# First head's k projected in the adaLN stage of a hybrid GLA and SSD layer

## The chip, the cores and the metric

The kernel runs on one core of a Trainium2 chip. The metric is the device time of one execution in microseconds; a profile is one execution recorded instruction by instruction. The engines are TensorE (PE, with its weight loads as PEld), VectorE (DVE), ScalarE (ACT), GpSimd (POOL) and the DMA queues; SyncE (SP) issues most transfers.

## The reference

One layer of a diffusion backbone over 512 latent tokens and 256 context tokens, width 1024, all in float32:

```
ada   = silu(c) @ w_ada + b_ada                    # six vectors of 1024; the same for c_ctx
h     = rms_norm(x) * (1 + scale1) + shift1        # context: its own scale and shift
parts = h @ w_in                                   # q, k, v, r, low-rank gates, z, xs, B, C, dt, gates a and b
y_a   = gated linear attention, both directions, 4 heads (dk 128, dv 256) @ w_pa
y_b   = Mamba-2 SSD, both directions, 32 heads in 4 groups @ w_pb
x     = x + g1 * ((sigmoid(gate_a)*y_a + sigmoid(gate_b)*y_b) @ w_out)
out   = rms_norm(x + g2 * swiglu(modulated rms_norm(x)))
```

The scans of the latent tokens start from the final states of the context tokens.

## The kernel before, in words

Every matrix product is done in three passes with operands split into a high and a low part: high by high, high by low, low by high. A weight block of 128x1024 comes by `load_w(key)`: SP loads it into one of three `raw` buffers (`load_raw`, line 176), ACT writes the high part `whi` (line 188), and DVE, later POOL, the low part `wlo` (line 189). `whi` and `wlo` have two buffers each. The names in a profile carry the key: `whi_k` is the high part of a head's k weights.

The start (lines 225 to 318) uses a pool `st`. The input x is normalised and transposed into `xnT`. The adaLN weights for shift1 and scale1 come in four blocks b of two loads `aw` of 1 MB each. `ada_first(b)` sums a block on PE (line 277, bank `ada`), copies it to `ar` on ACT (line 280) and turns it with four matmuls (line 283, bank `adaT`). `h_of(b)` then writes the normalised input's parts `hH` (ACT, line 299) and `hL` (DVE, line 301) for the contraction tiles 2b and 2b+1. The weights of `misc` (low-rank gates and dt) and of the first head's q are loaded ahead here, without priority.

When `st` is closed, the pools `pj` and `ch` are opened and take over its memory.

`proj_cols(key, with_ctx)` projects one 128-column block: for each of the eight contraction tiles three matmuls of 512 latent columns (lines 361, 362, 366, result `l_...`) and, with context, three of 256 columns (lines 364, 365, 368, result `c_...`). The results lie in banks of the tag `mm`, of which there are four; the tag `sm` has four more. `proj_rows` does v, r and z (lines 386 to 388, results `r_v`, `r_r`, `r_z`).

In program order, misc is projected first and copied into `M` (lines 394 to 398). From `M` and the small matrix `U` (read through `early_in`, a DMA of POOL, line 403) come the split operands `MS` (lines 413 to 415). The gate matmuls `pre` (line 469) follow, then the log-sigmoid `ge` on ACT and DVE (lines 471 to 474), its split `gh` and `gl` (lines 477, 478), and their way through DRAM (`gdr`). The dt values and their sums come next, and only then `gla_proj(0)`: q, k, v and r of head 0.

For each head h `gla_chain` runs the attention on the gates (`gc`, `kx`, `ky`, states `S`, levels `lv`, masks into `att`, outputs `o`, turned ones `oT`), while the projections of head h+1 fill PE between its steps. The chain's matmuls have high priority. Between the chains of heads 1 and 2, and again before that of head 3, `early_gate()` projects a pair of output gates (`l_ga`, `l_gb`) and writes them (`tg`) to DRAM (`tdr`). The four SSD groups follow, then the remaining output gates near 900 us, w_out and the FFN.

The other adaLN blocks (16 to 39 of 48, 128 columns each) are summed on POOL: `some_ada()` is called at certain weight blocks; every second call loads a block into a `raw` buffer (`raw_ada`) and POOL multiplies and adds it (lines 341 to 345); a one-column matmul ends it (line 336). Blocks that are left over run in the gate projections near 900 us.

The order of the instructions on each engine is fixed when the program is built, by a list scheduler that takes the first ready instruction in order of priority; each engine then runs its list in order and waits where an operand isn't there. `tc.high_priority()` lifts a part. `tc.issue_after(ins)` puts what is written inside it behind `ins` in the queue of its engine.

Of the kernel before, what the change touches and what calls it, by code (L numbers as in the profile page):

```python
# [14 lines left out]
P = 128  # L15
# [114 lines left out]
def hybrid_layer_kernel(ctx: ExitStack, tc: tile.TileContext, x, xc, wts, vec, rows, up, msk, lvl, out):  # L130
# [94 lines left out]
    with tc.tile_pool(name="st", bufs=1) as st:  # L225
        tcs = st.tile([P, KD, 2], F32, name="tcs")
        craw = vecs[:, V_CS:V_CS + 16].rearrange("p (k j) -> p k j", j=2)
        nc.scalar.activation(tcs, craw, AF.Tanh, scale=0.5)

        pre_ln = tc.keep_in_program_order(nc.scalar.preload_act_table_set("natural_log_exp_and_others"))  # L230
        nc.vector.scalar_tensor_tensor(cs, tcs, 1.0, craw, ALU.add, ALU.mult)
        nc.vector.tensor_scalar(cs, cs, 0.5, None, ALU.mult)

        csw = st.tile([P, KD, 32], F32, name="csw")
        nc.gpsimd.memset(csw, 0.0)
        nc.gpsimd.tensor_copy(csw[:, :, 0:2], cs)
        xs_ = [st.tile([P, D], F32, name=f"xt_{i}") for i in range(6)]
        xnT = st.tile([P, KD, NT], F32, name="xnT")
        mk = st.tile([P, M_TOT, P], F32, name="mk")

        def load_aw(b):
            ts = []
            for i in range(2):
                n = WIDX[("ada0", b, 2 * i)]
                raw = st.tile([P, 4, 512], F32, tag="aw", name=f"aw_{b}_{i}", bufs=6)
                nc.sync.dma_start(raw.rearrange("p (j k) c -> p j (k c)", j=2), wts[n:n + 2].rearrange("j p c -> p j c"))
                ts.append(raw)
            return ts

        def load_x(i):  # L250
            nc.sync.dma_start(xs_[i], x[i * P:(i + 1) * P, :] if i < 4 else xc[(i - 4) * P:(i - 3) * P, :])

        aw = [None] * 4
        nc.sync.dma_start(mk, msk)
        nc.vector.tensor_copy(idt, mk[:, M_ID, :])
        nc.gpsimd.tensor_copy(mkr, mk[:, 1:6, :])
        nc.gpsimd.tensor_copy(le8, mk[:, M_LE, :])

        sel = st.tile([P, 2], F32, name="sel")
        nc.vector.tensor_tensor(sel, mk[:, M_ID, 0:2], mk[:, M_ID, 32:34], ALU.add)  # L260
        for q in (64, 96):
            nc.vector.tensor_tensor(sel, sel, mk[:, M_ID, q:q + 2], ALU.add)
        for i in range(6):
            load_x(i)
        for b in range(4):
            aw[b] = load_aw(b)
        in_start[0] = True
        for key in (("misc",), ("q", 0)):
            ahead[key] = load_w(key)
        in_start[0] = False  # L270

        def ada_first(b):
            pt = sm_bank(f"ada_{b}")

            for k in range(KD):
                q = slice(32 * (k % 4), 32 * (k % 4) + 32)
                nc.tensor.matmul(pt[q, :], csw[:, k, :], aw[b][k // 4][:, k % 4, :], start=(k < 4), stop=(k >= 4))
            with tc.high_priority():
                ar = st.tile([P, 512], F32, tag="ar", name=f"ar_{b}", bufs=2)
                nc.scalar.activation(ar, pt, AF.Copy)  # L280
                pt = sm_bank(f"adaT_{b}")
                for j in range(4):
                    nc.tensor.matmul(pt[:, 2 * j:2 * j + 2], ar[:, j * P:(j + 1) * P], sel, start=True, stop=True)
                pv = pt[:, 0:8].rearrange("p (c j t) -> p c j t", c=2, t=2)
                k0 = 2 * b
                for c in range(2):
                    j0 = 8 * c + k0
                    nc.vector.tensor_tensor(ada[:, j0:j0 + 2, :], pv[:, c],
                                            vecs[:, V_BADA + j0:V_BADA + j0 + 2].unsqueeze(2).to_broadcast([P, 2, 2]), ALU.add)

                nc.vector.scalar_tensor_tensor(
                    s1[:, k0:k0 + 2, :], ada[:, 8 + k0:10 + k0, :], 1.0,
                    vecs[:, V_N1 + k0:V_N1 + k0 + 2].unsqueeze(2).to_broadcast([P, 2, 2]), ALU.add, ALU.mult)

        def h_of(b):
            for k in (2 * b, 2 * b + 1):
                for w, t0, n in ((0, 0, SEQ), (1, SEQ, CTX)):
                    xv = xnT[:, k, t0:t0 + n]
                    nc.scalar.activation(hH[:, k, t0:t0 + n], xv, AF.Identity, bias=ada[:, k, w:w + 1], scale=s1[:, k, w:w + 1])
                    nc.vector.tensor_scalar(xv, xv, s1[:, k, w:w + 1], ada[:, k, w:w + 1], ALU.mult, ALU.add)  # L300
                nc.vector.tensor_tensor(hL[:, k, :], xnT[:, k, :], hH[:, k, :].bitcast(F32), ALU.subtract)

        for i in range(6):
            sq = st.tile([P, D], F32, tag="sq", name=f"xsq_{i}")
            ss = sml.tile([P, 1], F32, tag="ss", name=f"xss_{i}", bufs=4)
            nc.scalar.activation(sq, xs_[i], AF.Square, accum_out=ss)
            r = rstd_of(ss, D, f"x{i}")
            nc.vector.tensor_scalar(xs_[i], xs_[i], r, None, ALU.mult)
            for half in range(2):
                pt = sm_bank(f"xT_{i}_{half}")  # L310
                for k in range(4):
                    kk = half * 4 + k
                    nc.tensor.transpose(pt[:, k * P:(k + 1) * P], xs_[i][:, kk * P:(kk + 1) * P], ident)
                nc.scalar.activation(xnT[:, half * 4:half * 4 + 4, i * P:(i + 1) * P],
                                     pt.rearrange("p (k t) -> p k t", t=P), AF.Copy)
        for b in range(4):
            ada_first(b)
            h_of(b)
# [30 lines left out]
    def proj_cols(key, with_ctx):  # L349
        if key[0] in ("q", "k") and key[1:2] != (0,):  # L350
            for _ in range(2):
                some_ada()
        if key[0] in ("ga", "gb"):
            some_ada()
        hi, lo = load_w(key)
        nm = "_".join(map(str, key))
        lat = mm_bank("l_" + nm)
        cx = mm_bank("c_" + nm) if with_ctx else None
        for k in range(KD):
            st, sp = k == 0, k == KD - 1  # L360
            nc.tensor.matmul(lat, hi[:, k, :], hH[:, k, 0:SEQ], start=st, stop=False)
            nc.tensor.matmul(lat, hi[:, k, :], hL[:, k, 0:SEQ], start=False, stop=False)
            if with_ctx:
                nc.tensor.matmul(cx[:, 0:CTX], hi[:, k, :], hH[:, k, SEQ:NT], start=st, stop=False)
                nc.tensor.matmul(cx[:, 0:CTX], hi[:, k, :], hL[:, k, SEQ:NT], start=False, stop=False)
            nc.tensor.matmul(lat, lo[:, k, :], hH[:, k, 0:SEQ], start=False, stop=sp)
            if with_ctx:
                nc.tensor.matmul(cx[:, 0:CTX], lo[:, k, :], hH[:, k, SEQ:NT], start=False, stop=sp)
        return lat, cx


    def proj_rows(keyf, ntile):
        banks = [mm_bank(f"r_{'_'.join(map(str, keyf(0)))}_{b}") for b in range(ntile // 2)]
        for kh in range(2):
            hi, lo = load_w(keyf(kh))
            if keyf(0)[0] in "vr":
                some_ada()
                some_ada()
            for i in range(ntile):
# [9 lines left out]
        return banks  # L389


    lat, cx = proj_cols(("misc",), True)
    M = pj.tile([P, NT], F32, tag="cva", name="M")
    nc.vector.memset(M[0:64, :], 1.0)
    for src, t0, n in ((lat, 0, SEQ), (cx, SEQ, CTX)):
# [26 lines left out]

    gnh = rsm[:, R_GN:R_GN + DV]
    nc.vector.tensor_scalar(gnh, gnh, 0.5, None, ALU.mult)


    def gla_proj_qk(h):
        lat, _ = proj_cols(("q", h), False)
        qT = pj.tile([P, SEQ], F32, tag="p3", name=f"qT_{h}")
        nc.scalar.activation(qT, lat, AF.Copy, scale=float(DK) ** -0.5)  # L430
        big = pj.tile([P, 3072], F32, tag="x12", name=f"kv_{h}")
        vt = big[:, 0:1536].rearrange("p (i c) -> p i c", c=DV)
        kt = big[:, 1536:2304].rearrange("p (i c) -> p i c", c=DK)
        kT = big[:, 2304:3072]
        lat, cx = proj_cols(("k", h), True)
        nc.scalar.activation(kT[:, 0:SEQ], lat, AF.Copy)
        nc.vector.tensor_copy(kT[:, SEQ:NT], cx[:, 0:CTX])
        for b, i0, n in ((0, 0, 4), (1, 4, 2)):
            pt = sm_bank(f"kt_{h}_{b}")
            for i in range(n):  # L440
                nc.tensor.transpose(pt[:, i * P:(i + 1) * P], kT[:, (i0 + i) * P:(i0 + i + 1) * P], ident)
            nc.scalar.activation(kt[:, i0:i0 + n, :], pt[:, 0:n * P].rearrange("p (i c) -> p i c", c=DK), AF.Copy)
        return qT, vt, kt, kT

    def gla_proj_vr(h, qT, vt, kt, kT):
        banks = proj_rows(lambda kh: ("v", h, kh), 6)
# [118 lines left out]
        nc.gpsimd.dma_start(cdr[d].rearrange("i h t -> (i h) t"), ct)  # L565
    ecum = cst.tile([P, 2, 4, 32], F32, name="ecum")
    nc.scalar.activation(ecum, cum, AF.Exp)
    pr = gla_proj(0)


    class Early:
# [643 lines left out]
```

## Time and profile before

| what | value |
|---|---|
| median of three runs | 1433.0 us (1431.25 to 1437.1) |
| profiled execution, its own time | 1428.55 us |
| its span, first to last instruction | 1426.7 us |
| PE busy | 1349.4 us, 95% |
| DVE, ACT, POOL busy | 881.1, 496.7, 476.1 us |
| mean granted clock of TensorE | 0.986 |

The profile's times count from the first instruction of the span. Busy time is a sum over instructions; an engine that is not on the chain that ends last may be idle at no cost.

### The profile page before, as it was taken

To read this page: it belongs to the slowest core of one execution; us is meant where nothing else is said; L and a number is where in the kernel's file an instruction comes from. 1 tells how busy PE (TensorE), PEld (TensorE's weight loads), DVE (VectorE), ACT (ScalarE), POOL (GpSimd) and SP (SyncE) were. 2 spreads that over 40 slices of the span, in tenths; PEclk is the share of its full clock that TensorE was granted. 3 is DMA by queue.
4 is the path that set the end of the run, shared out by engine and by line. 5 is a ranking of instruction groups with operands and counts; after the bars stand their busy time and mean duration, and the time that the engine had idled before them with its cause. 6 is when DMAs were issued, how large, how long until landed. Compare 5 with 4: busy or idle time off the path is not lost.

```text
span 1426.7 us, 19130 instructions
## 1 busy us (share of the span) xinstructions
PE 1349.4 (95%) x7462; PEld 1146.0 (80%) x7462; DVE 881.1 (62%) x1317; ACT 496.7 (35%) x825; POOL 476.1 (33%) x341
## 2 busy tenths in 40 slices
PE   5888999999998999998999989999889999999997
PEld 3687999889888778876887787778678888888886
DVE  4599757583595588558857975767683343433235
ACT  6464343433434132532332342332333323232222
POOL 1346555245423533343353324114641122100001
PEclk9998999999999999999999999999999999999999
DMA  9375433423422423323322333457423343333331
GB/s 370 123 259 151 128 102 111 126 93 126 122 75 67 141 98 101 97 73 90 104 82 89 96 97 101 158 184 267 135 87 109 113 122 115 120 116 93 100 106 72
DMA packets 71386, 175.49 MB, mean 123 GB/s; under 512 B 6384, under 2 KB 22912, under 8 KB 71168
## 3 DMA queue, kind: packets, MB, share of 16 engines
q1 hardware_dynamic: 57056, 161.11, 34.6%
q0 software_dynamic: 13952, 12.79, 3.8%
q8 instruction: 59, 0.97, 0.3%
q10 hardware_dynamic: 288, 0.36, 0.1%
q14 instruction: 31, 0.25, 0.1%
HBM read 159.37 MB, written 14.87 MB: 122 GB/s over the span
## 4 chain that ended last, share of the span: by engine, by line
PE 66%; DVE 16%; DMA 9%; issue 5%; ACT 2%; POOL 1%; SPq 0%; POOLq 0%; DVEq 0%; ACTq 0%
DMA E<-cdr 6%; PE up L1069 3%; PE gate L1068 3%; PE gate L1069 3%; PE up L1068 3%; PE gate L1067 3%; PE up L1067 3%; DVE E L830 3%; PE db L204 3%; PE db L206 3%; PE db L205 3%; PE lv L577 2%; PE pb_pb L716 2%; PE pb_pb L715 2%; PE pb_pb L717 2%
## 5 line engine op out<-in xcount | busy, mean ns | idle before, releaser
L341 POOL TENSOR_TENSOR raw_ada<-raw_ada,cs 128x1024 f32<-128x1024 f32 x32 | 69.7, 2180 | 265.3 <-DMA raw_ada<-in_wts_dram 230.4
L830 DVE TENSOR_TENSOR E<-E,ebias 128x512 f32<-128x512 f32 x64 | 68.8, 1077 | 51.0 <-DMA E<-cdr 50.8
L343 POOL TENSOR_TENSOR raw_ada<-raw_ada 128x512 f32<-128x512 f32 x64 | 80.0, 1250 | 3.7
L386 PE MATMUL r_z<-whi_z,hH 128*128 128x256 f32 x256 | 74.6, 291 | 5.8 <-DVE z L781 3.0
L388 PE MATMUL r_z<-whi_z,hL 128*128 128x256 f32 x256 | 73.4, 287 | 0.0
L387 PE MATMUL r_z<-wlo_z,hH 128*128 128x256 f32 x256 | 73.0, 285 | 0.0
L1067 PE MATMUL gate<-h2H,whi_gate 128*128 128x512 f32 (+1 forms) x192 | 72.2, 376 | 0.0
L1068 PE MATMUL gate<-h2L,whi_gate 128*128 128x512 f32 (+1 forms) x192 | 72.1, 376 | 0.0
L1069 PE MATMUL gate<-h2H,wlo_gate 128*128 128x512 f32 (+1 forms) x192 | 71.9, 374 | 0.0
L189 POOL TENSOR_TENSOR wlo_xs<-raw_xs,whi_xs 128x1024 fp32r<-128x1024 f32 x16 | 40.6, 2536 | 75.3 <-ACT whi_xs L188 75.3
L1069 PE MATMUL up<-h2H,wlo_up 128*128 128x512 f32 x160 | 63.0, 394 | 0.0
L1068 PE MATMUL up<-h2L,whi_up 128*128 128x512 f32 x160 | 62.4, 390 | 0.0
L1067 PE MATMUL up<-h2H,whi_up 128*128 128x512 f32 x160 | 62.3, 389 | 0.0
L189 DVE TENSOR_TENSOR wlo_down<-raw_down,whi_down 128x1024 fp32r<-128x1024 f32 x18 | 22.1, 1225 | 62.4 <-ACT whi_down L188 62.3
L189 DVE TENSOR_TENSOR wlo_gate<-raw_gate,whi_gate 128x1024 fp32r<-128x1024 f32 x20 | 31.7, 1584 | 45.6 <-ACT whi_gate L188 45.6
L170 POOL TENSOR_TENSOR rr_f<-rv_f,negh 128x1 f32<-128x1 f32 x4 | 2.6, 662 | 168.5 <-DVE rv_f L168 168.5
L386 PE MATMUL r_v<-whi_v,hH 128*128 128x256 f32 x192 | 56.4, 294 | 0.0
L189 POOL TENSOR_TENSOR wlo_z<-raw_z,whi_z 128x1024 fp32r<-128x1024 f32 x16 | 39.6, 2475 | 49.2 <-ACT whi_z L188 36.6
L387 PE MATMUL r_v<-wlo_v,hH 128*128 128x256 f32 x192 | 55.5, 289 | 0.0
L715 PE MATMUL pb_pb<-yT,whi_pb 128*128 128x512 f32 x128 | 55.3, 434 | 0.0
L388 PE MATMUL r_v<-whi_v,hL 128*128 128x256 f32 x192 | 55.3, 288 | 0.0
L205 PE MATMUL db<-wlo_down,fH 128*128 128x512 f32 x142 | 55.3, 389 | 0.0
(479 smaller groups left out, 4446.7 us busy)
## 6 DMA issues: line engine op xcount, KB each, us to landing
raw_ada<-in_wts_dram SPq DMA_DIRECT2D x32, 512.0 KB, 4.0
E<-cdr SPq DMA_DIRECT2D x64, 256.0 KB, 3.5
raw_gate<-in_wts_dram SPq DMA_DIRECT2D x22, 512.0 KB, 3.7
raw_up<-in_wts_dram SPq DMA_DIRECT2D x22, 512.0 KB, 3.5
raw_down<-in_wts_dram SPq DMA_DIRECT2D x22, 512.0 KB, 3.5
aw<-in_wts_dram SPq DMA_DIRECT2D x8, 1024.0 KB, 15.5
raw_xs<-in_wts_dram SPq DMA_DIRECT2D x16, 512.0 KB, 3.5
raw_z<-in_wts_dram SPq DMA_DIRECT2D x16, 512.0 KB, 3.6
```

The source lines that it names most:

```text
L189: (nc.gpsimd if split_pool[0] else nc.vector).tensor_tensor(lo, raw, hi.bitcast(F32), ALU.subtract)
L205: nc.tensor.matmul(out_, aH, bL, start=False, stop=False)
L341: nc.gpsimd.tensor_tensor(raw, raw, cs[:, :, 0:1].to_broadcast([P, KD, P]), ALU.mult)
L343: nc.gpsimd.tensor_tensor(raw[:, 0:n, :], raw[:, 0:n, :], raw[:, n:2 * n, :], ALU.add)
L386: nc.tensor.matmul(o, hH[:, kk, tk], hi[:, k, :], start=st, stop=False, skip_group_check=True)
L387: nc.tensor.matmul(o, hH[:, kk, tk], lo[:, k, :], start=False, stop=False, skip_group_check=True)
L388: nc.tensor.matmul(o, hL[:, kk, tk], hi[:, k, :], start=False, stop=sp, skip_group_check=True)
L715: nc.tensor.matmul(pt, hi[:, k, cl], aH[:, k, :], start=(k == 0), stop=False)
L830: nc.vector.tensor_tensor(ed, ed, ebias[:, d, n, hh].unsqueeze(2).to_broadcast([P, EH, P]), ALU.add)
L1067: nc.tensor.matmul(pts[kj][:, tk], hi[:, k, :], h2H[:, k, tk], start=(k == 0), stop=False)
L1068: nc.tensor.matmul(pts[kj][:, tk], hi[:, k, :], h2L[:, k, tk], start=False, stop=False)
L1069: nc.tensor.matmul(pts[kj][:, tk], lo[:, k, :], h2H[:, k, tk], start=False, stop=(k == KD - 1))
```

## The change

The first head's k weights are loaded and split with those of misc and q, into a tile `kw` of the pool `st` instead of the two buffers of `whi` and `wlo`. `gla_proj_qk(0)` is called right after misc is projected, before misc is copied to `M`. In the first head's q and k the matmuls from contraction tile 4 on, with all that `proj_cols` issues on PE behind them, are queued behind the last `adaT` matmul. The context result of the first head's k takes an `sm` bank. `ar` has one buffer instead of two. `some_ada()` isn't called in v of head 0, so its four calls fall away there and the blocks begin with r of head 0.

```diff
         for key in (("misc",), ("q", 0)):
             ahead[key] = load_w(key)
+        kw = st.tile([P, 2, KD, P], F32R, name="kw")
+        ahead[("k", 0)] = split_w(("k", 0), kw[:, 0], kw[:, 1])
         in_start[0] = False
+
+        ada_end = [None]
...
-                ar = st.tile([P, 512], F32, tag="ar", name=f"ar_{b}", bufs=2)
+                ar = st.tile([P, 512], F32, tag="ar", name=f"ar_{b}", bufs=1)
...
-                    nc.tensor.matmul(pt[:, 2 * j:2 * j + 2], ar[:, j * P:(j + 1) * P], sel, start=True, stop=True)
+                    ada_end[0] = nc.tensor.matmul(pt[:, 2 * j:2 * j + 2], ar[:, j * P:(j + 1) * P], sel, start=True, stop=True)
...
-        cx = mm_bank("c_" + nm) if with_ctx else None
+        cx = (sm_bank if key == ("k", 0) else mm_bank)("c_" + nm) if with_ctx else None
+        first = key in (("q", 0), ("k", 0))
         for k in range(KD):
             st, sp = k == 0, k == KD - 1
+            if first and k == 4:
+                wait_ada = tc.issue_after(ada_end[0].ins)
+                wait_ada.__enter__()
...
+        if first:
+            wait_ada.__exit__(None, None, None)
         return lat, cx
...
-            if keyf(0)[0] in "vr":
+            if keyf(0)[0] in "vr" and keyf(0)[:2] != ("v", 0):
                 some_ada()
                 some_ada()
...
     lat, cx = proj_cols(("misc",), True)
+    qk0 = gla_proj_qk(0)
     M = pj.tile([P, NT], F32, tag="cva", name="M")
...
-    pr = gla_proj(0)
+    pr = gla_proj_vr(0, *qk0)
```

The function `gla_proj_qk` itself is unchanged; it is only defined earlier.

## Rows read from the trace of the kernel before

**Rows 1.** The page: busy time of PE, and the chain that ended last.

```profile
span 1426.7 us, 19130 instructions
...
PE 1349.4 (95%) x7462; PEld 1146.0 (80%) x7462; DVE 881.1 (62%) x1317; ACT 496.7 (35%) x825; POOL 476.1 (33%) x341
...
PE 66%; DVE 16%; DMA 9%; issue 5%; ACT 2%; POOL 1%; SPq 0%; POOLq 0%; DVEq 0%; ACTq 0%
```

**Rows 2.** Windows: stretch, busy us of each engine (instructions), granted clock, DMA share, GB/s.

```profile
33.00:49.84 16.84, 16.36 (x86) 12.18 (x86) 7.37 (x13) 4.32 (x7) 4.38 (x4) 0.90 0.54 209
49.84:57.76 7.92, 5.48 (x18) 4.03 (x18) 5.30 (x11) 3.29 (x5) 1.70 (x3) 0.78 0.12 22
...
69.53:160.00 90.47, 80.45 (x567) 75.51 (x566) 83.91 (x124) 44.68 (x81) 48.48 (x40) 0.94 0.66 194
160.00:260.00 100.00, 100.00 (x703) 94.23 (x703) 62.93 (x109) 36.71 (x71) 50.59 (x41) 1.00 0.38 115
...
880.00:960.00 80.00, 80.00 (x372) 63.13 (x371) 57.36 (x90) 24.50 (x40) 13.84 (x15) 1.00 0.47 155
```

**Rows 3.** Timeline of PE, 48 to 70 us: start, us, instruction, [idle before <-releaser].

```profile
48.86 0.95 PE L283 MATMUL adaT<-sel,ar 128*128 128x2 f32 x8
...
53.10 0.80 PE L362 MATMUL l_misc<-hL,whi_misc 128*128 128x512 f32 x1 [1.05 <-DVE hL L301]
...
59.69 0.40 PE L361 MATMUL l_k<-hH,whi_k 128*128 128x512 f32 x1
...
64.47 0.28 PE L364 MATMUL c_k<-hH,whi_k 128*128 128x256 f32 x1
...
65.90 0.28 PE L364 MATMUL c_k<-hH,whi_k 128*128 128x256 f32 x1
67.22 1.16 PE L469 MATMUL pre<-U,MS 96*128 96x512 f32 x4 [1.04 <-issue]
68.22 0.28 PE L365 MATMUL c_k<-hL,whi_k 128*128 128x256 f32 x1
...
69.53 0.28 PE L386 MATMUL r_v<-whi_v,hH 128*128 128x256 f32 x1
```

**Rows 4.** Timeline of DVE, 49 to 70 us.

```profile
49.84 0.23 DVE L288 TENSOR_TENSOR ada<-adaT,vecs 128x4 f32<-128x4 f32 x2 [8.48 <-PE adaT L283]
...
55.04 0.70 DVE L394 MEMSET M<- 64x768 f32 x1 [0.22 <-DVE hL L301]
...
61.35 1.22 DVE L408 TENSOR_TENSOR U<-early_in,U 32x1024 fp32r<-32x1024 f32 x1 [1.58 <-ACT U L407]
...
64.47 2.55 DVE L415 TENSOR_TENSOR MS<-M,MS 32x768 fp32r<-32x768 f32 x1
...
68.69 1.38 DVE L415 TENSOR_TENSOR MS<-M,MS 32x768 fp32r<-32x768 f32 x1
```

**Rows 5.** Timelines of SP's queue, POOL and ACT, 16 to 63 us.

```profile
16.89 1.24 SPq L176 DMA_DIRECT2D raw_k<-in_wts_dram  x1
...
55.49 0.59 POOL L403 DMA_DIRECT2D early_in<-in_up_dram  x1 [8.56 <-DVE hL L301]
...
60.25 1.06 ACT L407 ACTIVATE U<-early_in 96x1024 fp32r<-96x1024 f32 x1 [2.23 <-DMA early_in<-in_up_dram]
...
62.90 0.60 ACT L430 ACTIVATE qT<-l_q 128x512 f32<-128x512 f32 x1
```

**Rows 6.** Timeline of PE, second head's q, 109 to 114 us.

```profile
109.21 0.80 PE L366 MATMUL l_q<-hH,wlo_q 128*128 128x512 f32 x1 [3.33 <-DVE wlo_q L189]
...
114.07 0.48 PE L362 MATMUL l_q<-hL,whi_q 128*128 128x512 f32 x1
```

**Rows 7.** Timelines of DVE, POOL and PE where the second head's chain ends.

```profile
246.51 0.74 DVE L674 COPY_PREDICATED att<-lvt,lv 128x512 f32<-128x512 uint8 x1
...
255.14 1.66 POOL L592 DMA_DIRECT2D g<-gdr  x2 [6.33 <-DMA tdr<-tg]
...
257.21 1.46 PE L577 MATMUL o<-S,qd 128*128 128x256 f32 x6
```

More of the change, by code (lines that the diff above doesn't have):

```diff
@@ L389, in proj_rows, with gla_proj_qk @@
         return banks
+    def gla_proj_qk(h):
+        lat, _ = proj_cols(("q", h), False)
+        qT = pj.tile([P, SEQ], F32, tag="p3", name=f"qT_{h}")
+        nc.scalar.activation(qT, lat, AF.Copy, scale=float(DK) ** -0.5)
+        big = pj.tile([P, 3072], F32, tag="x12", name=f"kv_{h}")
+        vt = big[:, 0:1536].rearrange("p (i c) -> p i c", c=DV)
+        kt = big[:, 1536:2304].rearrange("p (i c) -> p i c", c=DK)
+        kT = big[:, 2304:3072]
+        lat, cx = proj_cols(("k", h), True)
+        nc.scalar.activation(kT[:, 0:SEQ], lat, AF.Copy)
+        nc.vector.tensor_copy(kT[:, SEQ:NT], cx[:, 0:CTX])
+        for b, i0, n in ((0, 0, 4), (1, 4, 2)):
+            pt = sm_bank(f"kt_{h}_{b}")
+            for i in range(n):
+                nc.tensor.transpose(pt[:, i * P:(i + 1) * P], kT[:, (i0 + i) * P:(i0 + i + 1) * P], ident)
+            nc.scalar.activation(kt[:, i0:i0 + n, :], pt[:, 0:n * P].rearrange("p (i c) -> p i c", c=DK), AF.Copy)
+        return qT, vt, kt, kT
     lat, cx = proj_cols(("misc",), True)
+    qk0 = gla_proj_qk(0)
     M = pj.tile([P, NT], F32, tag="cva", name="M")
@@ L424, in hybrid_layer_kernel @@
     nc.vector.tensor_scalar(gnh, gnh, 0.5, None, ALU.mult)
[L427 to L443, printed above, removed]
     def gla_proj_vr(h, qT, vt, kt, kT):
```

## The prediction

> **What bounds the kernel now.** I read the page first. TensorE (PE) is busy 95% of the 1426.7 us span and holds 66% of the chain that ended last [rows 1], so the time is PE work plus PE's gaps and slow stretches. The windows show where those lie [rows 2]. Between 33 and 49.84 us PE is nearly full (16.36 of 16.84), from 49.84 to 57.76 it is busy 5.48 of 7.92 us at a granted clock of 0.78, from 69.53 to 160 us it is busy 80.45 of 90.47, and from 160 to 260 us it has no gap at all. VectorE (DVE) is the full engine of 69.53 to 160 us: 83.91 of 90.47. So there are two questions: how many PE microseconds the change moves into the gap of 49.84 to 57.76 us, and whether PE can keep that lead through a stretch that belongs to DVE.
>
> Then the timelines of PE, DVE, ScalarE (ACT), GpSimd (POOL) and the DMA queue over the first 70 us [rows 3 to 5]. The last adaLN sums (adaT, second row of time) end at 49.84 us; hL of the last block reaches PE at 53.10; the projection of the first head's k runs alone afterwards and v (`r_v`) starts at 69.53. Last the timeline of the second head's q, as the sample of a PE gap in DVE's stretch [rows 6], and the place where the second head's chain ends [rows 7], to see what the third chain waits for.
>
> **The change part by part.**
>
> *k's weights.* Their load is issued at 16.89 us already, a third raw buffer being free [rows 5], so no transfer moves. The split goes to a tile of its own (kw) and needs q's buffers no more: one ACT and one DVE instruction leave the front of the k projection for a stretch where ACT and DVE have room (ACT 4.32, DVE 7.37 busy of 16.84) [rows 2]. Counted as 0.
>
> *k's matmuls.* The pace of a 512-column matmul is (64.47-59.69)/21 = 0.228 us, of a 256-column one (65.90-64.47)/12 = 0.119 us [rows 3]. A k tile of misc or k has three of each: 1.04 us; one of q has three of the first: 0.684 us. All three projections are 8 x (1.04+0.684+1.04) = 22.1 us. Before 49.84 us PE does six tiles of misc and six of q: 10.35 us at that pace. In the new order misc 0 to 5, q 0 to 3 and k 0 to 3 (13.15 us) may run there, more than fits, so PE stays full up to the sums, which I leave at 49.84 us. What remains behind them is 22.1-10.35 = 11.8 us. Of that 2.8 us are tiles left over, and 1.37+2.08 us are q's and k's tiles 4 and 5: 6.25 us that need nothing later than 49.84, enough to cover the wait until hL is there (53.10 for tile 6). So all three projections end at 49.84+11.8 = 61.6 us. Before they end at 69.53 us, with four gate matmuls in between (67.22 to 68.22, 1.0 us) [rows 3]: **a lead of 69.53-1.0-61.6 = 6.9 us**.
>
> *The handover to v.* The four mm banks are then held by misc's two, q's and k's results. The copies out need tiles of pools that lie on the starting pool's memory (next part), so q's copy (0.60 us on ACT [rows 5]) starts only at 61.6 us and v at about 62.4. That costs 0.8 us: **6.1 us are left**.
>
> *What waits for the starting pool.* M's memset reads nothing, DVE had been idle for 8.48 us before 49.84, yet it runs at 55.04, right after the last hL; the first DMA of POOL (`early_in`) sat idle 8.56 us and left at 55.49 behind the same hL [rows 4, 5]. I read this as: the pools pj and ch come free as a whole, when the last reader of pool st is done. The new kw lies in st and its last reader is k's last matmul, so M, `early_in`, U, q's copy and k's copy all move from 55.5 to 61.6 us. For the gate chain (M, U, MS, `pre`) this is a delay. Upper bound: the whole 6.1 us, `pre` at 67.22+6.1 = 73.3. Lower bound: the DMA chain alone sets it: U's ACT instruction at 61.7+(60.25-55.49) = 66.5, U's two instructions 1.06+1.22 [rows 4, 5], `pre` at 68.9 with a little between them, that is +1.7. The copies into M and MS, which stand behind U on ACT today, fit into the flight of that DMA, but q's and k's copies are now ahead of them; I take +3. Nearer the lower bound, because U is what ACT stood still for (2.23 us).
>
> *What the delay costs at the end.* The gate chain feeds DVE's full stretch, so the first head's chain ends some 3 us later. PE does not stand still for it: from 160 to 260 us it is full [rows 2], with projections queued. The next chain ends with room: its last mask copy is over at 247.25, but the sums `o` that use it stand in PE's queue behind l_gb and run at 257.21; and POOL's loads of the third chain's gates wait for `tdr<-tg`, the output of the gate projections on PE [rows 7]. There the chain waits for PE, about 10 us, more than 3. So I cost the delay at 0 (bounds: 0 and +6.1).
>
> *ar with one buffer.* A block's copy to ar now waits for the adaT matmuls of the block before it, 0.95 us of PE [rows 3]; the blocks' matmuls come one after the other anyway, with the copies and sums between them. 0; paid in full for the last block, +0.95.
>
> *Late adaLN blocks.* Four calls fall out of v of head 0; every second call starts a block, so two of 24 blocks move behind the GLA heads, into the gate projections near 900 us. There POOL is busy 13.84 of 80 us and PE is full [rows 2]; the two loads of 512 KB and the POOL work behind them hide there. What stays keeps its place beside the projections, shifted by two blocks. 0; if PE had to wait once for a raw buffer, +1 to +4.
>
> The block that overlaps the gate chain costs DVE something: one MS subtraction took 2.55 us beside POOL's work, the other 1.38 us [rows 4]. The Trainium skill (SBUF — State Buffer, Who interferes with whom) says that a DVE instruction with two SBUF inputs is blocked whole by a GpSimd instruction that reads SBUF, which these rows agree with. By that rule two blocks fewer beside the first heads would give DVE at least 2 x 1.17 = 2.3 us back, and the sum would be about -8.4 if DVE set the end; by the rows of PE it stays at -6.1.
>
> **Sum.** -6.9 + 0.8 = -6.1 us. The profiled execution took 1428.55 us (1.85 around its span) and would become 1422.5; the median of the runs, 1433.0, lies 4.45 above it and becomes **1427 us**. What this kernel's measurement can tell from no change is about 0.5%, 7.2 us: 1425.8 and 1440.2.
>
> **Rivals.**
>
> B, *DVE takes the lead back.* If PE runs out of work that is ready between 69.5 and 160 us, where it already loses 10 us, it stops for the same DVE results and the lead becomes idle time. For it: DVE at 93% there, and the second head's q waited 3.33 us for its split on DVE [rows 6]. Against it: what PE lacks there is a position in a fixed queue, not work; v, r, q1, k1 and v1 do not need the gate chain. Time: 1433-6.1+6.1 to 1433+3 = 1433 to 1436.
>
> C, *slower: the gate chain sets the end.* One mechanism, the release of st: if the gates come the full 6.1 us later and the chains of the heads follow each other without slack, 1433+6.1 = 1439, and above 1440 if PE's clock falls once more in the longer waits. It decides once `pre` is later by more than the slack of about 10 us at 257 us minus the 6.1 us by which PE arrives there earlier: beyond some +4 us, `pre` after 71.2. Against it: that slack, and that POOL waits for PE's output there [rows 7].
>
> D, *more than the lead.* The wait for q1's split (3.33 us) leaves PE slow behind it: 11 matmuls from 109.21 to 114.07 us, 0.442 us each where 0.228 is the full pace [rows 6], so 11 x 0.214 = 2.4 us lost. If the earlier v lets the split come before PE wants it, both go: -6.1-3.3-2.4 = -11.8, 1421 us. For it: two loads fewer in the ring of raw buffers; against it: the split stays in DVE's full queue.
>
> E, *the change does not do what it says*: if the pools come free tile by tile, M and U do not wait for k, the gates come no later and v starts at 61.6: -6.9, 1426 us. Hardly to be told from the forecast by time.
>
> **How the numbers follow.** Forecast (with E) 0.52, its own range 1423 to 1430 (bank handover 0 to 2 us, leftovers of the queue order); B 0.20; C 0.12; D 0.16. Faster by over 0.5% is D and 0.4 of the forecast: 0.37. Slower by over 0.5% is somewhat over half of C and a tail of B: 0.09. The rest, 0.54, is within 0.5%. The range leaves out the far half of C and some of D: 1418 to 1438 us.
>
> **What the new profile would show.** Right: no PE gap between 49.8 and 61 us and a granted clock near 1 there; k's last matmul near 61.6; M's memset and `early_in` behind it, not behind hL; v's first matmul near 62.5; `pre` at 69 to 71; the second head's q earlier by about 6 us, and the third chain's gate loads (255.14 us now) too. Wrong: the sums adaT later than 50 us because k's tiles stand before them; v waiting for banks until M is copied; PE's idle time in 70 to 160 us up from 10 to 16 us (B); those gate loads no earlier (B) or later (C).

## The result and the profile after

The change makes the kernel slower, by half a percent. Its median is 1440.6 us (1437.4 to 1443.7), that of the kernel before on the same chip 1433.7: a ratio of 1.0055, with a 95% interval of 1.0033 to 1.0077. The forecast was 1427. The profiled execution took 1443.69 us, the longest of its six, and that of before 1428.55, shorter than all six beside it: the two profiled executions lie 15.1 us apart where the medians lie 7 to 8 apart. The traces tell where time goes, the ratios how much.

The windows of after, in the stretches of [rows 2] and three more (stretch, busy us of PE, PEld, DVE, ACT and POOL, granted clock, DMA share, GB/s):

```profile
33.00:49.84 16.84, 16.84 (x79) 12.67 (x80) 8.46 (x14) 5.23 (x8) 0.00 (x0) 0.80 0.52 210
49.84:57.76 7.92, 7.92 (x49) 7.02 (x48) 3.99 (x9) 2.50 (x4) 0.00 (x0) 1.00 0.01 3
...
69.53:160.00 90.47, 79.06 (x545) 74.11 (x544) 75.37 (x110) 47.16 (x85) 52.89 (x44) 0.94 0.63 190
160.00:260.00 100.00, 97.03 (x669) 89.87 (x668) 74.84 (x125) 37.15 (x68) 47.42 (x38) 1.00 0.41 122
260.00:300.00 40.00, 36.61 (x182) 31.19 (x181) 20.65 (x42) 17.13 (x38) 9.71 (x7) 0.91 0.19 51
300.00:345.00 45.00, 41.70 (x266) 38.28 (x266) 28.77 (x43) 13.69 (x25) 17.32 (x14) 0.96 0.29 94
```

The same view of before for the two stretches that [rows 2] leave out:

```profile
260.00:300.00 40.00, 39.94 (x209) 34.10 (x208) 27.03 (x53) 19.34 (x38) 11.07 (x9) 1.00 0.31 92
300.00:345.00 45.00, 44.27 (x327) 41.94 (x327) 26.35 (x41) 14.70 (x29) 25.07 (x18) 1.00 0.29 97
```

The gap of 49.84 to 57.76 us is filled, at full clock, as intended; before it, from 33 to 49.84 us, the granted clock was 0.80 (0.90 before). But PE is then idle 11.41 us in 69.53 to 160 (10.02 before), 2.97 in 160 to 260 (none), 3.39 in 260 to 300 (0.06) and 3.30 in 300 to 345 (0.73): 10.3 us more, in part at the lower clock.

PE's timeline of after at the ends of the move (answers to [rows 3]):

```profile
62.44 0.28 PE L376 MATMUL c_k<-hH,kw 128*128 128x256 f32 x1
63.77 0.38 PE L396 MATMUL r_v<-whi_v,hH 128*128 128x256 f32 x1 [1.06 <-ACT qT L405]
...
74.51 0.38 PE L396 MATMUL r_v<-whi_v,hH 128*128 128x256 f32 x1 [2.65 <-DVE M L428]
...
76.92 1.16 PE L480 MATMUL pre<-U,MS 96*128 96x512 f32 x4 [0.35 <-DVE MS L445]
```

v starts 5.8 us earlier, then stands still for 2.65 us in the middle, because its next bank is held until misc's result is copied to M. The gate matmuls `pre` come 9.7 us later. The timelines of DVE, POOL and ACT say why (answers to [rows 4, 5]):

```profile
52.16 0.23 DVE L292 TENSOR_TENSOR ada<-adaT,vecs 128x4 f32<-128x4 f32 x2 [9.71 <-PE adaT L287]
...
56.18 0.96 DVE L305 TENSOR_TENSOR hL<-xnT,hH 128x768 fp32r<-128x768 f32 x1
...
63.98 0.70 DVE L424 MEMSET M<- 64x768 f32 x1
...
69.87 2.33 DVE L438 TENSOR_TENSOR U<-early_in,U 32x1024 fp32r<-32x1024 f32 x1 [3.19 <-ACT U L437]
72.23 1.50 DVE L443 CAST MS<-M 32x768 fp32r<-32x768 f32 x1
...
75.67 2.09 DVE L445 TENSOR_TENSOR MS<-M,MS 32x768 fp32r<-32x768 f32 x2
...
84.21 0.69 DVE L485 SCALAR_TENSOR_TENSOR ge<-pre,ge 128x512 f32<-128x512 f32 x1
```

```profile
63.31 0.57 POOL L433 DMA_DIRECT2D early_in<-in_up_dram  x1 [45.09 <-ACT whi_v L188]
...
69.22 1.90 POOL L345 TENSOR_TENSOR raw_ada<-raw_ada,cs 128x1024 f32<-128x1024 f32 x1 [4.24 <-DMA raw_ada<-in_wts_dram]
...
68.77 1.06 ACT L437 ACTIVATE U<-early_in 96x1024 fp32r<-96x1024 f32 x1 [4.56 <-DMA early_in<-in_up_dram]
69.86 0.59 ACT L427 ACTIVATE M<-l_misc 16x512 f32<-16x512 f32 x1
```

M's memset no longer follows the last hL (over at 57.1) but k's last matmul (62.7). The 9.7 us are: `early_in` leaves 7.8 later; it takes 0.7 longer to arrive (5.46 us to U's ACT instruction, 4.76 before); U's subtraction takes 1.1 longer (2.33 for 1.22), beside a late adaLN block on POOL; and between the end of that subtraction and `pre` lie 4.7 us as before, because the copies into M and MS still stand behind U in the queues of ACT and DVE. The first `ge` stood at 73.62 before and is 10.6 later.

The next chains carry it. The output norm of head 0 and the output step of head 1, on DVE:

```profile
201.58 0.17 DVE L168 TENSOR_SCALAR rv_o<-oss 128x4 f32<-128x4 f32 x1
206.56 1.66 DVE L706 SCALAR_TENSOR_TENSOR on<-o,rr_o,rw 128x256 f32<-128x256 f32 x4 [4.80 <-POOL rr_o L170]
...
269.38 1.66 DVE L706 SCALAR_TENSOR_TENSOR on<-o,rr_o,rw 128x256 f32<-128x256 f32 x4 [1.15 <-POOL rr_o L170]
```

Before, these stood at 184.93, 188.96 and 262.75. Of the 16.7 us that head 0's chain ends late, 9.9 are there when its masks begin (`dg`, at 153.97 for 144.06), and 7.9 more arise between `dg` and its first output matmul `o`, in 36.52 us for 28.62 (before, then after; windows as above, and DVE's group of `ek` in them):

```profile
144.06:172.68 28.62, 26.90 (x229) 26.70 (x228) 24.93 (x40) 9.13 (x14) 14.52 (x11) 1.00 0.43 124
153.97:190.49 36.52, 34.97 (x250) 32.19 (x248) 32.64 (x46) 11.31 (x17) 25.97 (x20) 1.00 0.42 127
L667 DVE TENSOR_TENSOR ek<-ek,kv 128x512 f32<-128x512 f32 x5 | 3.4, 680 | 0.0
L678 DVE TENSOR_TENSOR ek<-ek,kv 128x512 f32<-128x512 f32 x5 | 6.7, 1340 | 0.0
```

DVE had more to do there: the splits of the third head's q, k and v fell into this stretch (before, only two splits of the second head's r), and so did five late blocks on POOL for three, beside which single `ek` steps took up to 2.39 us for 0.68. No run takes these apart.

PE reached the third chain's gate projections early (POOL's `g<-gdr` at 252.47, 255.14 in [rows 7]) and then waited for `on`; its waits between 160 and 300 us are led by

```profile
PE oT L588 <- DVE on L706: 4.1, 3, 2.5
```

(total us, times, longest), where before there was none. Some 2.7 us of lead were there at 250 us and were waited away.

### The profile page after: what moved, and what is told of

Its sections match the earlier page's. It is cut to its first block, busy times and chain, and to the rows that moved or that the text cites. A ratio compares the mean times of both kernels' runs of the same rounds, so it can differ in the third digit from the quotient of the medians.

```text
span 1441.9 us, 19139 instructions
## 1 busy us (share of the span) xinstructions
PE 1355.6 (94%) x7462; PEld 1151.1 (80%) x7462; DVE 880.4 (61%) x1317; ACT 497.3 (34%) x825; POOL 473.5 (33%) x341
## 4 chain that ended last, share of the span: by engine, by line
PE 60%; DVE 18%; DMA 10%; issue 6%; POOL 3%; ACT 2%; SPq 1%; POOLq 0%; DVEq 0%; ACTq 0%
DMA E<-cdr 6%; PE up L1080 3%; PE gate L1079 3%; PE up L1079 3%; PE gate L1080 3%; PE gate L1078 3%; PE up L1078 3%; PE db L204 3%; PE db L205 3%; PE db L206 3%; DVE E L841 2%; DVE cv_x L757 2%; PE pb_pb L727 1%; PE pb_pb L726 1%; PE pb_pb L728 1%
## 5 line engine op out<-in xcount | busy, mean ns | idle before, releaser
L345 POOL TENSOR_TENSOR raw_ada<-raw_ada,cs 128x1024 f32<-128x1024 f32 x32 | 65.3, 2042 | 237.3 <-DMA raw_ada<-in_wts_dram 215.4
L841 DVE TENSOR_TENSOR E<-E,ebias 128x512 f32<-128x512 f32 x64 | 65.3, 1023 | 57.6 <-DMA E<-cdr 57.5
L347 POOL TENSOR_TENSOR raw_ada<-raw_ada 128x512 f32<-128x512 f32 (+1 forms) x64 | 81.0, 1266 | 3.7
L189 DVE TENSOR_TENSOR wlo_down<-raw_down,whi_down 128x1024 fp32r<-128x1024 f32 x18 | 22.0, 1225 | 62.4 <-ACT whi_down L188 62.3
L844 ACT ACTIVATE E<-E 128x512 f32<-128x512 f32 x32 | 20.2, 632 | 110.1 <-DVE E L843 86.1
L396 PEld LDWEIGHTS r_z<-whi_z,hH 128*128 128x128 f32 x256 | 50.1, 196 | 7.4 <-issue 4.7
```

The lines of the kernel that those rows point to most:

```text
L189: (nc.gpsimd if split_pool[0] else nc.vector).tensor_tensor(lo, raw, hi.bitcast(F32), ALU.subtract)
L345: nc.gpsimd.tensor_tensor(raw, raw, cs[:, :, 0:1].to_broadcast([P, KD, P]), ALU.mult)
L347: nc.gpsimd.tensor_tensor(raw[:, 0:n, :], raw[:, 0:n, :], raw[:, n:2 * n, :], ALU.add)
L396: nc.tensor.matmul(o, hH[:, kk, tk], hi[:, k, :], start=st, stop=False, skip_group_check=True)
L841: nc.vector.tensor_tensor(ed, ed, ebias[:, d, n, hh].unsqueeze(2).to_broadcast([P, EH, P]), ALU.add)
```

## The experiments

All ratios are to the kernel before on the same chip, with the 95% interval.

**Who delays the gates: the pool, the sums, or the late blocks?** T1 is rival C's mechanism, the release of pool st; R2 the sums behind k's tiles 0 to 3; R3 the late blocks.

*kw_split* and *split2*: k's late tiles out of st, so that st is released at the last hL. The main lines of split2:

```diff
     hL = hpool.tile([P, KD, NT], F32R, name="hL")
+    kx = hp.enter_context(tc.tile_pool(name="kx", bufs=1, side="right"))
+    kw2 = kx.tile([P, 2, 3, P], F32R, name="kw2")
...
-        kw = st.tile([P, 2, KD, P], F32R, name="kw")
+        kw = st.tile([P, 2, 5, P], F32R, name="kw")
```

In kw_split four tiles lie in `kw2`, in cst, in place of `low_pad` and `top_pad`, two unused tiles that only shift what lies behind them.

> As the changed kernel, but only k's tiles 0 to 3 of the split weights lie in the start pool; tiles 4 to 7 (4 KB a partition) lie in the constant pool, in the place of the two pads, so that the start pool no longer waits for k's last matmul. T1 (the loss is the late release of the start pool): the memset of M back from 63.98 to 55-59 us, early_in issued there too, the first pre from 76.92 to 68-72, and the time at 1425-1433 us. What stays of the delay then is that misc's last matmuls end at 61.6 (57.2 before). R2 (k's tiles 0 to 3 ahead of the last adaLN sums cost it): these stand where they stood, so 1439-1442. R3 (the late adaLN blocks cost it): they begin late here too, so 1439-1442.

Measured: 1.0076 (1.0048 to 1.0103). M's memset came back as T1 said (57.67 us), the gates most of the way (`pre` at 73.1, a microsecond beyond T1's range, first `ge` at 78.3), and the time did not.

*no_kw* drops the two lines of `kw`. *k_behind* puts all of k behind the sums. *late_back* restores the calls in v.

```diff
-            if first and k == 4:
+            if first and k == (0 if key[0] == "k" else 4):
...
-            if keyf(0)[0] in "vr" and keyf(0)[:2] != ("v", 0):
+            if keyf(0)[0] in "vr":
```

> As the changed kernel, but without k's early split: its weights come through the two rotating buffers as before, so k runs only when they are there, all of it behind the sums, and the start pool is not held. T1: memset of M at 55-57 us, pre at 67-70, time 1430-1435 (no PE lead and no late gates). R2: 1430-1435 as well, as k is behind the sums. R3: the late blocks still begin late, 1438-1441.

> As the changed kernel, but all eight k tiles stand behind the last adaLN sums on PE, not only tiles 4 to 7. R2: the sums end at 50 us again instead of 51.98, hH and hL come 2 us earlier, and the time falls to 1430-1435. T1: k's weights are read until 63-65 us all the same, so the start pool is released as late, pre stays at 76-79 and the time at 1439-1443. R3: 1439-1442.

> As the changed kernel, but the late adaLN blocks begin in the first head's v again, as before. R3: with the two blocks back in v the time falls to 1430-1435. T1: pre stays at 76-78 us and the time at 1439-1443; R2: the same.

Measured: no_kw 1.0019 (0.9997 to 1.0041), k_behind 1.0036 (1.0016 to 1.0056), late_back 1.0068 (1.0045 to 1.0092). The late blocks are not the loss. R2 is at most a part: k_behind's interval overlaps that of the change. In k_behind the sums end at 49.4 us, and `early_in` still leaves at 63.39 (63.31 in the change): the sums' place doesn't set the release. Its `pre` comes at 73.52 and its first `ge` at 79.3 all the same, because there ACT's and DVE's queues hold the copies into M and MS ahead of U, for the most part within the flight of `early_in`:

```profile
64.82 0.59 ACT L427 ACTIVATE M<-l_misc 16x512 f32<-16x512 f32 x1 [0.76 <-DVE M L426]
70.50 1.57 DVE L445 TENSOR_TENSOR MS<-M,MS 32x768 fp32r<-32x768 f32 x1
72.10 1.37 DVE L438 TENSOR_TENSOR U<-early_in,U 32x1024 fp32r<-32x1024 f32 x1
```

> As kw_split (the start pool holds k's split weights for the early tiles only), but with tiles 5 to 7 (3 KB a partition) in a small pool beside hH and hL, so that no other tile of the kernel changes its address: the pads are back. Theory now: two things delay the chains of heads, T1 the late release of the start pool (the gates), T2 the output norm of head 0, whose 1.04 us step on POOL stands in POOL's queue behind a late adaLN block (DVE's output step waited 8.59 us for it in kw_split, 3.87 before). T1 and T2: the gates come as in kw_split (first ge at 78 us), the norm waits 8 to 9 us again, chain 1 starts at 203-205 us, and the time is 1436-1440, because what kw_split lost in the feed-forward stage (matmuls of 395 ns for 389) came with the moved addresses. Rival: the addresses do nothing, and it is 1441-1444 like kw_split.

Measured: 1.0005 (0.9991 to 1.0019). DVE's timeline of split2:

```profile
57.34 0.70 DVE L433 MEMSET M<- 64x768 f32 x1 [0.27 <-DVE hL L312]
...
77.80 1.29 DVE L494 SCALAR_TENSOR_TENSOR ge<-pre,ge 128x512 f32<-128x512 f32 x2 [6.31 <-ACT ge L493]
```

With the other tiles in their places the early release takes the whole loss away: T1 holds, at 0.5%. *before_pad* tests the other half, addresses alone:

```diff
-    cst.tile([P, 104], F32, name="low_pad")
+    cst.tile([P, 108], F32, name="low_pad")
```

> The kernel before with one unused tile 16 bytes a partition longer, so that every tile behind it moves by 16 bytes: same instructions, other addresses. Theory A: some groups of matmuls take 395 ns for 389, as in kw_split and the three kernels with the norm on DVE, and the time is 1438-1446. Theory B: addresses are nothing, 1433-1437.

Measured: 1.0066 (1.0041 to 1.0090). So moved tiles alone can cost what kw_split lost; the rows are in the last section.

**Why the lead buys nothing once the gates are back.** In split2 head 0's norm (`rv_o` on DVE at 187.35) waited 8.81 us for its one step on POOL:

```profile
192.25 1.90 POOL L352 TENSOR_TENSOR raw_ada<-raw_ada,cs 128x1024 f32<-128x1024 f32 x1 [4.56 <-DMA raw_ada<-in_wts_dram]
194.23 1.26 POOL L354 TENSOR_TENSOR raw_ada<-raw_ada 128x512 f32<-128x512 f32 x1
195.45 1.04 POOL L170 TENSOR_TENSOR rr_o<-rv_o,negh 128x4 f32<-128x4 f32 x1
```

POOL idles for a late block's weights with the norm queued behind it. T2 says that this is what eats the lead. Four kernels take the step to DVE:

```diff
+        if name[0] == "o":
+            a = sml.tile([P, w], F32, tag="ra", name=f"ra_{name}", bufs=1)
+            nc.vector.tensor_scalar(a.bitcast(I32), v.bitcast(I32), 1, None, ALU.logical_shift_right)
+            nc.vector.tensor_scalar(r.bitcast(I32), a.bitcast(I32), -1.0, 1597463007.0, ALU.mult, ALU.add)
+            for _ in range(3):
+                nc.vector.tensor_tensor(a, r, r, ALU.mult)
+                nc.vector.scalar_tensor_tensor(a, a, -0.5, v, ALU.mult, ALU.mult)
+                nc.vector.scalar_tensor_tensor(r, a, 1.5, r, ALU.add, ALU.mult)
+            return r
```

> split2, and the output norm of the heads computed on DVE (eleven small steps of a reciprocal square root, some 0.16 us each, in the place of the power on POOL), so that it stands behind no late block. T2: DVE's output step follows 2 us behind the sums instead of 8.6, chain 1 starts at 197-200 us, PE's wait for oT near 195 is gone, and the time falls to 1429-1434. If only T1 holds, or PE's own work bounds that stage: as split2.

> The changed kernel with the output norm of the heads on DVE, the start pool held as in the change. T1: the gates stay at 84 us and chain 0 ends at 200 as before this edit; the norm's wait of 4.80 us falls to 2, so chain 1 starts 3 us earlier at most (210) and the time is 1436-1440. T2 alone (the norm is the whole loss): 1430-1434.

> The kernel before with the output norm of the heads on DVE. PE was busy 100 of 100 us from 160 to 260 there, so an output step 2 us earlier has nothing to fill: both theories say 1431-1435, no difference. If the chains of heads bound the kernel before too, 1427-1430.

Measured: 1.0081 (1.0053 to 1.0109), 1.0109 (1.0080 to 1.0138) and 1.0073 (1.0050 to 1.0096): all slower, the kernel before too. The new tile `ra` moves every tile behind it, so these three tell nothing of T2. *split2_dve2* rotates the scratch through the buffers of `rv` instead.

> split2_dve without its new tile: the scratch of the norm on DVE rotates through buffers that were there, so that no tile moves. Theory A (what split2_dve lost late came with the moved tiles: its last stage's matmuls took 395 ns for 389): chain 1 starts near 197 us as there, those matmuls are at 389 again and the time is 1430-1436. Theory B (DVE's eleven small steps and what they collide with cost it): 1441-1446, as split2_dve.

Measured: 1.0028 (1.0014 to 1.0041), between the two theories. The tile `ra` cost some 0.5%. The norm's wait is gone (the output step at 188.92 for 196.53) and chain 1 starts 6 us earlier, yet the kernel gains nothing over split2: PE then waits 3.9 us for head 1's `on` and 3.6 for `ek`. T2, as the one cause, falls.

*split2_noq2* and *split2_kb*: no blocks begun in the third head's q and k; all of k behind the sums, as in k_behind.

```diff
-        if key[0] in ("q", "k") and key[1:2] != (0,):
+        if key[0] in ("q", "k") and key[1:2] not in ((0,), (2,)):
```

> split2 with no late adaLN blocks begun in the third head's q and k (they come four calls later), so that the output norm of head 0 finds POOL free. T2 (the norm behind a late block, 8.6 us in the kernels with an early release): it waits 1 to 4 us, PE's 4.4 us wait for oT is gone, chain 1 starts at 198-200, and the time is 1429-1434. If PE's own work or the chain of head 1 bounds it: as split2, 1435-1438.

> split2 with all eight k tiles behind the last adaLN sums, as in k_behind. The sums come 2 us earlier and misc ends 2.6 us earlier than in the change, so the first ge comes at 75-76 us (78 in split2, 73.6 before). T1 with a price of 0.7 us a us: 1433-1435; if the norm's wait at chain 0's end swallows it: as split2.

Measured: split2_noq2 1.0044 (1.0023 to 1.0065), a miss: from head 1's output step on it ran 2 to 4 us ahead of the kernel before, up to 880 us, but four late blocks were then still to do, and PE waited there. Its waits between 880 and 1040 us:

```profile
PE ob L205 <- DVE wlo_out L189: 6.4, 3, 2.6
PE l_gb L383 <- DVE wlo_gb L189: 2.5, 1, 2.5
PE pb_pb L737 <- DVE wlo_pb L189: 1.7, 1, 1.7
```

split2_kb: 0.9994 (0.9972 to 1.0015), no difference with the first `ge` at 72.54, earlier than before; the chain of head 0 still ended 6.6 us later. It had reached its masks (`dg`) at 142.26, 1.8 us earlier than before, and then took 35.8 us to the first `o`, with the third head's q and k split among them.

*late_only* is the late start of the blocks (not in v of head 0) on the kernel before; *split2_late* undoes it in split2; *v1* is split2_kb with the late start undone and split2_noq2's skip, so two blocks stay late; *v2* begins these two in the first state-space group.

```diff
-        if key[0] in ("q", "k") and key[1:2] not in ((0,), (2,)):
+        if key[0] in ("q", "k") and key[1:2] not in ((0,), (2,)) or key in (("bm", 0), ("cm", 0)):
```

> The kernel before with one part of the change alone: the late adaLN blocks begin two blocks later, not in the first head's v. Theory L (blocks left at the gate stage cost there): the last two blocks stand near 890 to 915 us, where PE was full from 880 to 960; they cost 1 to 4 us and the time is 1434-1438. Rival: two blocks fewer beside the first head's gates free DVE there, the chain starts 1-2 us earlier, 1430-1433.

> split2 with the late blocks begun in the first head's v, as before. Theory L: no block is left after 355 us, the gate stage gives back 1 to 4 us, and the time is 1431-1435 (split2 1435). Rival (their place beside the gates costs more): 1436-1440.

> split2_kb with the late blocks begun in the first head's v as before and none begun in the third head's q and k: as many blocks are late as in the change (two left at the gate stage), but none stands ahead of the first head's output norm on POOL. Theory N (the norm's wait eats PE's lead): the norm waits under 3 us, chain 1 starts at 197-199 us, the state-space stage is 3-4 us ahead of before as in split2_noq2, and the gate stage takes 1-4 us back: 1429-1434. Rival: the chains of heads 1 to 3 set the pace whatever chain 0 does: 1434-1437.

> v1, and two late blocks begun in the first state-space group's projections, so that none is left at the gate stage. Theories N and L together: the 3-4 us of lead reach the end, 1426-1431. If the blocks collide with DVE in the state-space stage: 1433-1437.

Measured: late_only 0.9995 (0.9976 to 1.0015); split2_late 1.0040 (1.0023 to 1.0056), a miss whose cause is open; v1 **0.9937** (0.9913 to 0.9961), v2 **0.9940** (0.9917 to 0.9964), medians 1427.8 and 1427.0 us. Both are faster than either kernel. v2 leaves no block to the gate projections near 900 us and v1 two: these two cost nothing that can be measured.

Two more kernels ask which part earns that: *before_noq2* is the skip on the kernel before; *v1_held* is v1 with all of `kw` in st again.

> The kernel before with no late blocks begun in the third head's q and k, the rest of it as it was. Theory G (the early k earns the gain, the blocks only stood in its way): PE had no wait between 160 and 300 us before, so nothing is gained there, and two blocks left at the gate stage cost up to 3 us: 1434-1438. Rival (the blocks' place is the whole gain of v1): 1425-1429.

> v1 with all of k's split weights in the start pool, as the change has them, so that the pool is released at k's last matmul. T1 (the release delays the gates and with them every chain): first ge at 79-81 us, against 73.6 in v1, and 1433-1437, some 5 to 8 us over v1. Rival (only the third head's blocks ahead of the norm made the late gates matter): 1427-1430 as v1.

Measured: before_noq2 1.0018 (0.9998 to 1.0039), v1_held 1.0025 (1.0005 to 1.0045). The blocks' place alone gains nothing, and holding st costs v1 all of its gain, 0.9%. In v1_held the first `ge` came at 76.26 us, earlier than its 79 to 81. DVE of v1:

```profile
73.61 0.69 DVE L494 SCALAR_TENSOR_TENSOR ge<-pre,ge 128x512 f32<-128x512 f32 x1 [4.95 <-ACT ge L493]
...
187.88 1.66 DVE L715 SCALAR_TENSOR_TENSOR on<-o,rr_o,rw 128x256 f32<-128x256 f32 x4
...
257.45 1.66 DVE L715 SCALAR_TENSOR_TENSOR on<-o,rr_o,rw 128x256 f32<-128x256 f32 x4 [1.15 <-POOL rr_o L170]
```

The gates are where they were before, and head 1's output step is 5.3 us earlier than before, by nearly the forecast's lead. In v1_held it stands at 261.03. These two traces show where steps stand and not what they earn: the profiled execution of v1 took 1433.3 us, the longest of its six, that of v1_held 1428.3, the shortest of its twelve.

## Why the prediction was wrong

**The step that failed** is the delay of the gates, in size, and with it the zero that it was costed at. The text took `pre` 3 us later (bounds 1.7 and 6.1), and said that rival C decides beyond some 4 us. `pre` came 9.7 us later, outside the bounds. The direction is C's, and it was given 12% because of the 3. That C's 1439 lies near the 1440.6 measured is partly luck: it was worked out from gates 6.1 us late. That the release of st makes the loss is shown twice (split2 against the change, v1 against v1_held). The mechanism was read rightly from M's memset and `early_in` in [rows 4, 5]; the path from there to `pre` was not. Of the 6.7 us between the forecast's 70.2 and the 76.92 measured:

- 3.3 us lie behind U. The text let the copies into M and MS fit into the flight of `early_in` and put `pre` right behind U's subtraction, at 68.9, and added little more than 1 us for them. In the fixed queues of the change they stayed behind U, as before, and took 4.7 us (72.20 to 76.92). k_behind shows the order that the text had in mind, and `pre` at 73.52.
- 1.6 us are the release. k's last matmul ended at 62.7 for 61.6, and `early_in` left at 63.31 for 61.7. PE had no gap from 33 us to there; what was slower was its granted clock from 33 to 49.84 us (0.80 for 0.90). The sums did come 2.3 us later (52.16 for 49.84), because k's tiles 0 to 3 stand before them, as the list of wrong signs allowed, but k_behind shows that this didn't move the release.
- 1.8 us are the flight of `early_in` (0.7) and U's subtraction (1.1), which now met a late block on POOL.

**The slack of 10 us** of [rows 7] was no slack of the whole chain. Head 0's chain ended 16.7 us later (201.58 for 184.93) from gates 10.6 us late, while in the trace DVE's work for the third head fell into its masks, and head 1's output step 6.6 us later. The early PE shortens the slack at the same time; the text counted that, and with a delay of 9.7 the sum turns.

**Right:** the filled gap and its clock; k's last matmul (62.7 for 61.6); v at 63.8 for 62.4, so a lead of 69.53-1.0-63.77 = 4.8 us where 6.1 was forecast; the late blocks at 0 (late_only 0.9995). E is out, since M waited for k. The handover was costed at 0.8 us and took 1.06 and 2.65, so that r of head 0 began 2.7 us early (86.2 for 88.9). ar's single buffer was not tried alone.

**B and D:** PE's idle time in 69.53 to 160 us rose by 1.4 us only, so B did not take the lead there; it was lost at the ends of the chains, after 160 us, where DVE's extra work in head 0's masks is B's cause in another place. D's wait for q's split is not among after's waits, and the third head's v began 8.9 us early (193.4 for 202.3), yet the gain never reached the end.

**A lead of the forecast's size can be had, in another kernel.** With the gates in time and the third head's late blocks out of the way, v1 is 0.63% faster (0.39 to 0.87%, some 5.6 to 12.5 us, where 6.1 was forecast for the change). Neither condition alone does it: split2_kb 0.9994, v1_held 1.0025, before_noq2 1.0018. v1 differs from split2_kb in two edits, the blocks begun in v again and none in the third head's q and k; they were not tried apart on split2_kb, so which of them frees the lead is not shown.

**Open:** by which of its waits the blocks of the third head eat the lead (the norm on POOL in split2, `ek` on DVE in split2_kb); why split2_late loses 0.4% where v1 begins its blocks in v too; how the 0.9% between v1 and v1_held divides, since their traces put the first `ge` only 2.7 us apart (73.61 and 76.26), in executions whose granted clock differed at the start (0.80 and 0.97 in 33 to 49.84 us).

## What to carry to other kernels

When work moves ahead in the fullest engine's queue, ask what it now holds back: here a weight tile in a pool released as a whole held the longest chain by 8 us, for a lead of 5. Draw the bounds of such a delay along the whole path to the first consumer, transfer and neighbours included, and not from the release alone; and take work as fitting into a wait only if the queue holds it ahead of that wait. A lead counts only if the chain that the engine meets next is early too; and work in small blocks on a side engine has to be placed anew when the chains move against it.

## What the runs showed of the hardware

A shift of every tile behind one pad by sixteen bytes a partition cost 0.66% with the same instructions. The groups of one FFN product, before and then before_pad (engine, operation, count | busy us, mean ns):

```profile
L1069 PE MATMUL up<-h2H,wlo_up 128*128 128x512 f32 x160 | 63.0, 394 | 0.0
L1068 PE MATMUL up<-h2L,whi_up 128*128 128x512 f32 x160 | 62.4, 390 | 0.0
L1067 PE MATMUL up<-h2H,whi_up 128*128 128x512 f32 x160 | 62.3, 389 | 0.0
```

```profile
L1069 PE MATMUL up<-h2H,wlo_up 128*128 128x512 f32 x160 | 64.0, 400 | 0.0
L1067 PE MATMUL up<-h2H,whi_up 128*128 128x512 f32 x160 | 63.2, 395 | 0.0
L1068 PE MATMUL up<-h2L,whi_up 128*128 128x512 f32 x160 | 63.2, 395 | 0.0
```

The groups of `up` and `gate` grow by 5 us in sum (`gate` 216.2 to 218.5), of the 9.3 us between the medians; the granted clock is 1.00 in both from 1100 to 1300 us. In kw_split it was the same groups; in the three kernels with the tile `ra` those of `db` (395 for 389). In the change, split2, v1 and v1_held all these groups have the means of before. What in the address does it, and where the rest of the 9.3 us lies, was not tried.

DVE instructions with two SBUF inputs ran longer beside POOL: in split2 one took 2.39 us that takes 0.69 without:

```profile
312.92 1.90 POOL L352 TENSOR_TENSOR raw_ada<-raw_ada,cs 128x1024 f32<-128x1024 f32 x1 [2.51 <-DVE eq L678]
312.98 2.39 DVE L680 TENSOR_TENSOR eq<-eq,qT 128x512 f32<-128x512 f32 x1
```

2.39-0.69 = 1.70 us is nearly the POOL instruction's 1.90. The Trainium skill (SBUF — State Buffer, Who interferes with whom) has the later of the two wait for the whole of the other, and the rows agree. Before, that step had run at 309.88, just ahead of POOL's instruction, in 0.69 us. PE waited 2.9 us for `ek` between 300 and 330 us in split2 and 0.7 before.
